# One decoder step (SSD, HGRN2 and two MLPs): the order of the engines' instructions comes from the scheduler's other machine model

## The chip, the cores and the metric

The kernel runs on one NeuronCore of one Trainium2 chip. Five engines work on it, each through its own list of instructions, in the order of that list: TensorE (PE, matrix products into PSUM), VectorE (DVE), ScalarE (ACT), GpSimdE (POOL) and SyncE (SP, which here only issues DMA transfers). They wait for one another through semaphores. The metric is the device time of one launch in microseconds (us), lower is better.

## The reference, cut to what matters

The step takes 512 prompt tokens of one new sequence and 32 sample tokens (8 sequences of 4 tokens), each a row of 1024 numbers, through two layers in float32:

```
h = x
h += ssd_mixer(rmsnorm(h))        # 32 heads of 64, 4 groups, state 64x128 per head
h += squared_relu_mlp(rmsnorm(h)) # 1024 -> 4096 -> 1024
h += hgrn_mixer(rmsnorm(h))       # 8 heads of 128
h += squared_relu_mlp(rmsnorm(h))
y = rmsnorm(h)
```

`ssd_mixer` multiplies by a 1024 x 5152 matrix, runs a causal convolution of width 4 and a SiLU over 3072 of the columns, scans the result along time in chunks (decays as differences of a cumulative sum, products inside a chunk, a state carried from chunk to chunk), multiplies by SiLU of a gate z, normalises each of 4 groups and multiplies by a 2048 x 1024 matrix. `hgrn_mixer` multiplies by 1024 x 4096, scans per head with a forget gate for each key dimension, normalises each head, gates and multiplies by 1024 x 1024. The new states are outputs too.

## The kernel before, in words

All 544 tokens (512 + 32) stay on chip; activations lie with features on the 128 partitions and tokens along the row, in 8 tiles `x[k]` of 128 x 544. The weights stream through in **units** of 128 x 1024: `raw<u>` is loaded by SP (L171) into one of three buffers, then split into a rounded part `whi` (ACT, L188 or L209) and a remainder `wlo` (DVE, L189; every third unit of the first layer on ACT and POOL, L230 and L233). A product runs as three passes, high x high, high x low and low x high, so a unit is 48 matmuls (L316, tiles `ps`, `po`, `pm`, `pd`, `pho`). Each product of a unit fills one of only **two** PSUM accumulators (`acc_tile`, pool `psb`, bufs=2): the product of unit n+2 cannot start until something has read the product of unit n. In the MLPs seven half-size products (L1020) stand for eight.

In the SSD layer the units come in the order of a list (ORDER, L35): gate units z (read by ACT `thz`, L511, and then by DVE `zs`, L512), input units i (read by three ACT copies into `pre`, L472 to L474, under high priority) and output units o (added to `x`, L405). After `pre` come `cacc` (ACT L480, three DVE steps L482), `th` (ACT L485) and the result (`xs`, `BC`, L486 and L489). `cacc` has one buffer, `pre` and `th` two.

Between the matmuls of the units runs **background** work, written as generators that give way after so many matmuls (PACE, L38): `scan` for each of 4 groups g, `gated_norm` behind it, and in the HGRN layer `levels` (tiles `pa`, at spans 1, 2, 4 ... 64 of a head) and `states` (`pk`, `pS`, `pz`, `po`, `pn`, `pt`). In `scan`, `rows(c)` has SP load a broadcast of the cumulative sums into `w<g>_<c>` (512 KB in 4 KB rows), and `weights(c)` turns it into decays on ACT: two L574 (`E`, only for c > 0), eight L576, one L577. `w`, the sample states `st`, and `bm` share six buffers of the tag "st", so a load of a `w` can have to wait until a state has been written out (L753) or until a matmul has read an older tile.

```
rows:     w = pool.tile([P, 8, P], F32, tag="st", bufs=6, ...)          # L563
          nc.sync.dma_start(w, cum_d[hs, c * P : (c + 1) * P].partition_broadcast(P))   # L564
weights:  nc.scalar.activation(w[:, h], w[:, h], AF.Relu, ...)          # L576, 8 times
          nc.scalar.activation(w, w, AF.Exp, scale=-1.0)                # L577
silu2:    nc.scalar.activation(v3(th), z, AF.Tanh, scale=0.5)           # L511
          nc.vector.scalar_tensor_tensor(v3(zs), v3(th), 1.0, z, ADD, MUL)   # L512
```

At the end of the HGRN layer the chain of the last head (7) runs `pa7_8`, `pa7_16`, `pa7_32`, `pa7_64` (L1159, L1178), `pk7` (L1250), `pS7` (L1262), `pz7`, `po7` (L1285, L1287), the norm of the head (`o`, `oms`, `nwr`, L1293 to L1302), `pt7` (L1316), `g7`, `oh7` and `ol7`, and then the output products `pho1_*` that read `oh7` and `ol7`. The output products of heads 0 to 3 are `pho0_*`.

The program traces all of this in Python order. Then the tile framework's scheduler sorts the instructions of each engine: it walks through a model of the machine, picks the next instruction that the model says can start, with the traced order and the priorities (`tc.high_priority()`) behind it, and sets semaphore waits to fit. What each engine runs, and on which tiles, is fixed by the trace; where each instruction stands in its engine's list is the scheduler's. The context that does this is opened in `_build`, L1536.

Of the kernel before, what the change touches and what calls it, by code (L numbers as in the profile page):

```python
# [1528 lines left out]
def _build(arrays):  # L1529
    import concourse.bacc as bacc  # L1530

    nc = bacc.Bacc("TRN2", target_bir_lowering=False, num_devices=1)
    io = {n: nc.dram_tensor(f"in_{n}", v.shape, mybir.dt.from_np(v.dtype), kind="ExternalInput").ap() for n, v in arrays.items()}
    for n, s in _OUT.items():
        io[n] = nc.dram_tensor(f"out_{n}", s, F32, kind="ExternalOutput").ap()
    with tile.TileContext(nc) as tc:  # L1536
        trunk(tc, io)
    return nc

# [21 lines left out]
```

## Time and profile before

| what | value |
|---|---|
| median of 3 runs | 1568.02 us (1567.37 to 1571.41) |
| the profiled execution, its own time | 1573.07 us |
| its span, first to last instruction | 1571.3 us |
| mean granted TensorE clock | 0.991 |
| PE busy | 1541.0 us, 98% of the span |
| DVE busy | 1092.6 us, 70% |
| ACT busy | 769.5 us, 49% |
| POOL busy | 121.0 us, 8% |

In the profile "L316" is line 316 of the kernel; "out<-in" names the tiles that an instruction writes and reads, without their numbers. A wait is the idle time of an engine just before an instruction, with what released it. "PEclk" is the clock that the throttle granted TensorE, 1.00 being full speed. Times in a timeline count from the start of the span. Windows give the busy time of each engine in a stretch.

### The profile page before, as it was taken

The page shows a single profiled execution, that of the slowest core. Times are in us where ns is not written, and L with a number is a line of the kernel's source. Part 1 is how long each engine was busy: PE and PEld are TensorE (multiplying, and loading weights), DVE is VectorE, ACT ScalarE, POOL GpSimd, SP SyncE. Part 2 cuts the span into 40 slices and gives each one's busy share as a digit, 9 for nine tenths or more (in the row PEclk, how much of TensorE's full clock was granted, in tenths as well). Part 3 has the DMA queues.
Part 4 walks back from the last instruction along what each step waited for, and adds up shares of the span by engine and source line. Part 5 has one row for each costly group of instructions (what it writes and reads, how often), then busy time and mean ns, then how long its engine had stood idle before and what let it go on. Part 6 is the DMA issues. An engine that isn't in the chain of part 4 may idle for free.

```text
span 1571.3 us, 32703 instructions
## 1 busy us (share of the span) xinstructions
PE 1541.0 (98%) x13420; PEld 1478.6 (94%) x13420; DVE 1092.6 (70%) x2142; ACT 769.5 (49%) x1506; POOL 121.0 (8%) x195
## 2 busy tenths in 40 slices
PE   8998899999999999999999999999999999999997
PEld 7997889898999999999999999999999999999996
DVE  7888797969778656464555878888878656474544
ACT  5686666675345436273554333333345446273552
POOL 4211010100001001010000000000001001010001
PEclk9999899999999999999999999999999999999998
DMA  6465456474446245453323232233226245363311
GB/s 195 123 172 161 131 140 180 121 215 123 139 100 174 90 118 148 111 161 92 110 63 108 69 99 83 89 105 110 70 91 180 81 128 141 108 167 94 103 55 58
DMA packets 86342, 188.94 MB, mean 120 GB/s; under 512 B 12784, under 2 KB 33168, under 8 KB 86192
## 3 DMA queue, kind: packets, MB, share of 16 engines
q1 hardware_dynamic: 73120, 164.21, 33.2%
q0 software_dynamic: 11808, 21.50, 8.6%
q8 instruction: 105, 1.72, 0.5%
q10 hardware_dynamic: 1264, 1.14, 0.2%
q14 instruction: 45, 0.37, 0.1%
HBM read 169.64 MB, written 17.18 MB: 119 GB/s over the span
## 4 chain that ended last, share of the span: by engine, by line
PE 87%; DMA 2%; DVE 2%; ACT 1%; issue 1%; POOL 0%; POOLq 0%; SPq 0%; ACTq 0%
PE pd L316 24%; PE ps L316 23%; PE pp L1020 11%; PE pm L316 6%; PE po L316 5%; PE pc L1020 5%; PE pho L316 3%; DMA w<-cum_d 1%; PE pa L1159 1%; PE py L608 1%; DMA raw<-in_W 1%; PE pu L599 1%; PE pi L620 1%; DVE wlo L189 1%; PE pS L1262 1%
## 5 line engine op out<-in xcount | busy, mean ns | idle before, releaser
L188 ACT CAST whi<-raw 128x512 fp32r<-128x512 f32 x318 | 195.1, 618 | 396.3 <-PE pd L316 155.2
L189 DVE TENSOR_TENSOR wlo<-raw,whi 128x512 fp32r<-128x512 f32 x318 | 218.4, 689 | 101.3 <-ACT whi L188 99.0
L316 PE MATMUL pd<-gh,whi 128*128 128x272 f32 x992 | 205.8, 288 | 0.0
L316 PE MATMUL pd<-gl,whi 128*128 128x272 f32 x992 | 205.3, 288 | 0.0
L316 PE MATMUL pd<-gh,wlo 128*128 128x272 f32 x992 | 205.1, 288 | 0.0
L316 PEld LDWEIGHTS pd<-gh,whi 128*128 128x128 f32 x992 | 156.0, 188 | 0.0
L316 PEld LDWEIGHTS pd<-gh,wlo 128*128 128x128 f32 x992 | 155.7, 188 | 0.0
L316 PEld LDWEIGHTS pd<-gl,whi 128*128 128x128 f32 x992 | 155.5, 188 | 0.0
L316 PE MATMUL ps<-uh_s,whi 128*128 128x272 f32 x576 | 127.0, 302 | 8.8 <-DVE zs L512 8.7
L316 PE MATMUL ps<-ul_s,whi 128*128 128x272 f32 x576 | 122.4, 294 | 0.0
L316 PE MATMUL ps<-uh,whi 128*128 128x272 f32 x512 | 112.6, 300 | 0.0
L316 PEld LDWEIGHTS ps<-uh_s,whi 128*128 128x128 f32 x576 | 92.9, 194 | 14.9 <-issue 13.2
L316 PE MATMUL ps<-ul,whi 128*128 128x272 f32 x512 | 106.5, 289 | 0.0
L316 PE MATMUL ps<-uh,wlo 128*128 128x272 f32 x512 | 106.2, 289 | 0.0
L405 DVE TENSOR_TENSOR x<-pd,x 128x544 f32<-128x544 f32 x62 | 44.8, 723 | 87.8 <-PE pd L316 87.8
L316 PEld LDWEIGHTS ps<-ul_s,whi 128*128 128x128 f32 x576 | 93.2, 194 | 0.3
L181 POOL DMA_DIRECT2D v<-in_W x48 | 42.1, 1068 | 599.7 <-DMA v<-in_W 373.4
L316 PE MATMUL ps<-uh_s,wlo 128*128 128x272 f32 x576 | 86.1, 290 | 0.0
L316 PEld LDWEIGHTS ps<-uh,whi 128*128 128x128 f32 x512 | 80.8, 189 | 3.7 <-issue 1.4
L316 PEld LDWEIGHTS ps<-ul,whi 128*128 128x128 f32 x512 | 80.4, 189 | 0.0
L316 PEld LDWEIGHTS ps<-uh,wlo 128*128 128x128 f32 x512 | 80.1, 188 | 0.0
L316 PEld LDWEIGHTS ps<-uh_s,wlo 128*128 128x128 f32 x576 | 78.3, 190 | 0.2
(428 smaller groups left out, 3810.4 us busy)
## 6 DMA issues: line engine op xcount, KB each, us to landing
raw<-in_W SPq DMA_DIRECT2D x198, 512.0 KB, 3.6
v<-in_W SPq DMA_DIRECT2D x48, 256.0 KB, 4.4
v<-in_W POOLq DMA_DIRECT2D x48, 256.0 KB, 5.6
wlo<-in_W POOLq DMA_DIRECT2D x34, 256.0 KB, 5.9
w<-cum_d SPq DMA_DIRECT2D x16, 512.0 KB, 7.3
st<-in_ssm_in SPq DMA_DIRECT2D x16, 512.0 KB, 5.5
out_ssm_s<-st SPq DMA_DIRECT2D x16, 512.0 KB, 4.9
a<-in_W SPq DMA_DIRECT2D x24, 256.0 KB, 4.0
```

The lines of the kernel that those rows point to most:

```text
L181: nc.gpsimd.dma_start(raw[:, c : c + 512], io["W"][u + 1][:, :512], accum_op=ADD)
L188: nc.scalar.copy(hi, raw)
L189: (eng or nc.vector).tensor_tensor(lo, raw, hi.bitcast(F32), SUB)
L316: nc.tensor.matmul(ps[:, h, :HF], block(a, c0 + k * step), o[:, h * HF : (h + 1) * HF], start=(first and i == 0), stop=(last and i == len( ...
L405: nc.vector.tensor_tensor(v3(x[m]), ps[:, :, :HF], v3(x[m]), ADD)
L599: nc.tensor.matmul(pu, bt[:, c], xts[c].rearrange("p h q -> p (h q)"), start=True, stop=True)
L608: nc.tensor.matmul(py[64 * (h % 2) : 64 * (h % 2) + 64, (h // 2) * P : (h // 2 + 1) * P], xds[c][:, h], ws_[c][:, h], start=True, stop=True,)
L620: nc.tensor.matmul(pi[:, j * P : (j + 1) * P], hT[:, j * P : (j + 1) * P], CT[:, cs], start=True, stop=True)
L1020: nc.tensor.matmul(ps, block(w, k * P), o, start=(name_ in ("p1", "p2", "q7") and k == 0 and j == 0), stop=(k == 3 and j == 2), skip_group ...
L1159: nc.tensor.matmul(pv4[b * NS : (b + 1) * NS, c], K[:, bs], QQ[:, 2 - n :, bs], start=True, stop=True, tile_position=(0, b * NS),)
L1262: nc.tensor.matmul(pS[:, c * P : (c + 1) * P], kt[:, c], vt[:, c], start=True, stop=True)
```

## The change

One argument is added where the tile context is opened:

```diff
-    with tile.TileContext(nc) as tc:
+    with tile.TileContext(nc, schedule_with_timeline_sim=True) as tc:
```

With it the scheduler uses its second machine model, which follows the engines' queues in time, to decide which instruction of an engine comes next. The instructions and their tiles are the same; each engine runs the same set, in another order, and the semaphore waits follow that order. Rows of PE change in 4858 lines of difference on some 6600 rows, of ACT in 1581 on some 1370. Three places follow; in the rows the number behind a unit's name (ps14) is the unit, or the group and chunk (w1_0), and the last number only tells buffers apart.

**ACT, in the SSD layer, around the copies of unit 14's product (pre17)**, which free the accumulator that unit 16's product (ps16) takes. Before:

```order
L188 CAST whi16_1_1707<-raw16_1434 128x512
L726 ACTIVATE bm0_1627<-bq0_1597,seqrow_123 128x128
L472 COPY pre17_1686<-ps14_1566 128x272
L473 COPY pre17_1686<-ps14_1566 128x240
L474 COPY pre17_1686<-ps14_1566 128x8x4
L726 ACTIVATE bm0_1627<-bq0_1597,seqrow_123 128x128
L480 ACTIVATE cacc7_1549<-pre7_1542,vh_129 128x568
L726 ACTIVATE bm0_1627<-bq0_1597,seqrow_123 128x128 x3
L576 ACTIVATE w1_0_2131<-w1_0_2131,tok_754 128x128 x5
```

Now:

```order
L726 ACTIVATE bm0_1627<-bq0_1597,seqrow_123 128x128 x8
L188 CAST whi17_1_1807<-raw17_1560 128x512
L230 ACTIVATE wlo18_1814<-raw18_1704 128x1024
L720 ACTIVATE ws0_1602<-ws0_1602 32x256
L576 ACTIVATE w1_0_2131<-w1_0_2131,tok_754 128x128 x8
L577 ACTIVATE w1_0_2131<-w1_0_2131 128x1024
L472 COPY pre17_1686<-ps14_1566 128x272
L473 COPY pre17_1686<-ps14_1566 128x240
L474 COPY pre17_1686<-ps14_1566 128x8x4
```

The copies stood ahead of all work on w1_0 and now stand behind all nine instructions of it. On PE the matmuls py0_3, whose end lets the load of w1_0 be issued, stood ahead of the end of unit 14's product; now they stand behind the end of unit 15's, with only psi0 and two of pn0 between them and ps16.

**ACT, a little later, around thz16**, the first reader of unit 16's product; ps18 takes its accumulator. Before:

```order
L574 ACTIVATE E1_1_2255<-w1_1_2142 64x512 x2
L576 ACTIVATE w1_1_2142<-w1_1_2142,tok_754 128x128 x7
L188 CAST whi19_1_1992<-raw19_1804 128x512
L576 ACTIVATE w1_1_2142<-w1_1_2142,tok_754 128x128
L485 ACTIVATE th21_1799<-cacc21_1794 128x568
L511 ACTIVATE thz16_1893<-ps16_1818 128x544
L577 ACTIVATE w1_1_2142<-w1_1_2142 128x1024
L574 ACTIVATE E1_2_2382<-w1_2_2174 64x512 x2
```

Now:

```order
L574 ACTIVATE E1_2_2382<-w1_2_2174 64x512
L373 ACTIVATE ssq_94<-y0_1158 128x544
L574 ACTIVATE E1_2_2382<-w1_2_2174 64x512
L577 ACTIVATE w1_1_2142<-w1_1_2142 128x1024
L188 CAST whi19_1_1992<-raw19_1804 128x512
L576 ACTIVATE w1_2_2174<-w1_2_2174,tok_754 128x128 x8
L485 ACTIVATE th17_1698<-cacc17_1693 128x568
L577 ACTIVATE w1_2_2174<-w1_2_2174 128x1024
L480 ACTIVATE cacc21_1794<-pre21_1787,vh_129 128x568
L485 ACTIVATE th21_1799<-cacc21_1794 128x568
L511 ACTIVATE thz16_1893<-ps16_1818 128x544
```

thz16 stood behind the work on w1_1 and ahead of that on w1_2; now it stands behind both, and th17 and cacc21, which stood ahead of w1_1, have moved behind w1_2 as well.

**PE, at the end of the HGRN layer, in head 7's chain from pS7 on.** Before:

```order
L316 MATMUL pho0_2_0_14432<-oh3_10176,wlo154_1_14342 128x272 x2
L1262 MATMUL pS7_14457<-vt7_14166,kt7_14415 128x128 x4
L316 MATMUL pho0_2_1_14469<-oh0_10170,whi154_0_14339 128x272 x2
L316 MATMUL pho0_2_1_14469<-ol0_10171,whi154_0_14339 128x272 x2
L316 MATMUL pho0_2_1_14469<-oh0_10170,wlo154_0_14341 128x272 x2
L316 MATMUL pho0_2_1_14469<-oh1_10172,whi154_0_14339 128x272 x2
L316 MATMUL pho0_2_1_14469<-ol1_10173,whi154_0_14339 128x272 x2
L316 MATMUL pho0_2_1_14469<-oh1_10172,wlo154_0_14341 128x272 x2
L1272 MATMUL pz7_14482<-hst7_14408,qm7_14417 32x128 x8
```

Now:

```order
L316 MATMUL pho1_0_1_14671<-oh6_10182,wlo156_1_14549 128x272 x2
L1250 MATMUL pk7_14410<-ident_77,K7_13890 128x128 x4
L1262 MATMUL pS7_14457<-vt7_14166,kt7_14415 128x128 x4
L1272 MATMUL pz7_14482<-hst7_14408,qm7_14417 32x128 x8
L1275 MATMUL pz7_14482<-ident_77,K7_13890 128x128
L1285 MATMUL po7_14509<-vt7_14166,att7_13921 128x128 x2
L1287 MATMUL po7_14509<-S7_14462,q7_13800 128x128
L1285 MATMUL po7_14509<-vt7_14166,att7_13921 128x128
L1287 MATMUL po7_14509<-S7_14462,q7_13800 128x128
L1285 MATMUL po7_14509<-vt7_14166,att7_13921 128x128
L1289 MATMUL pzs7_14517<-zi7_14492,h_sel_10154 32x128
```

Where the matmuls of pho0 stood between the steps of head 7's chain, all of pho0 and the parts of pho1 that do not read head 7 now stand ahead, and the steps from pk7 to pts7 follow one another directly.

## The prediction

> **What bounds the kernel now.** I read the page first: busy times, the chain that ended last, the transfers.
>
> ```profile
> PE 1541.0 (98%) x13420; PEld 1478.6 (94%) x13420; DVE 1092.6 (70%) x2142; ACT 769.5 (49%) x1506; POOL 121.0 (8%) x195
> ...
> PE 87%; DMA 2%; DVE 2%; ACT 1%; issue 1%; POOL 0%; POOLq 0%; SPq 0%; ACTq 0%
> ...
> w<-cum_d SPq DMA_DIRECT2D x16, 512.0 KB, 7.3
> ```
>
> PE is busy for 1541.0 of 1571.3 us. The matmuls stay the same ones, so an order of instructions can give back at most the 30 us in which PE is idle, and can cost any amount: every place counts at which PE would wait. Next, PE's waits.
>
> ```profile
> PE ps L316 <- DVE zs L512: 8.7, 1, 8.7
> PE gn_pc L351 <- DVE ssq L377: 2.4, 2, 1.7
> PE ps L316 <- DVE xl L369: 2.2, 3, 1.5
> ...
> PE po L316 <- ACT pre L474: 0.8, 1, 0.8
> ```
>
> One wait stands out: 8.7 us before a unit's product, for `zs`, the reader that frees one of the two accumulators. What it costs beside itself shows in the windows around it and around the 1.7 us wait of `gn_pc`.
>
> ```profile
> 150.00:155.00 5.00, 1.80 (x15) 1.58 (x13) 0.00 (x0) 3.77 (x10) 0.00 (x0) 1.00 0.82 294
> 155.00:160.00 5.00, 0.00 (x0) 0.00 (x0) 4.79 (x11) 4.50 (x10) 0.00 (x0) 0.69 0.73 217
> 160.00:165.00 5.00, 3.78 (x17) 3.54 (x17) 3.68 (x6) 5.00 (x12) 0.00 (x0) 0.63 0.82 295
> 165.00:170.00 5.00, 5.00 (x32) 5.00 (x32) 3.01 (x14) 0.94 (x2) 0.00 (x0) 0.71 0.08 33
> 170.00:175.00 5.00, 5.00 (x41) 5.00 (x40) 1.44 (x3) 2.87 (x6) 1.25 (x2) 0.95 0.32 92
> ...
> 255.00:260.00 5.00, 5.00 (x26) 5.00 (x26) 2.24 (x12) 3.43 (x7) 0.52 (x3) 0.57 0.83 194
> 260.00:265.00 5.00, 5.00 (x44) 5.00 (x43) 2.29 (x4) 2.90 (x7) 0.00 (x0) 1.00 0.32 113
> ```
>
> The second last column but two is the granted clock. In 155 to 160 PE does nothing, and afterwards does 32 matmuls in 5 us where it does 44 at a clock of 1.00: over 160 to 175 the low clock costs some 3.3 us. The clock also falls around 255 (26 matmuls instead of 44, 2 us), after no more than the 1.7 us wait.
>
> Last, ACT and SP around that stall.
>
> ```profile
> 127.40 0.39 ACT L472 COPY pre<-ps 128x272 f32<-128x272 f32 x1
> 127.68 0.37 ACT L473 COPY pre<-ps 128x240 f32<-128x240 f32 x1
> 127.93 0.21 ACT L474 COPY pre<-ps 128x32 f32<-128x32 f32 x1
> ...
> 130.00 1.58 ACT L576 ACTIVATE w<-w,tok 128x128 f32<-128x128 f32 x5
> ...
> 133.01 1.06 ACT L577 ACTIVATE w<-w 128x1024 f32<-128x1024 f32 x1
> ...
> 151.18 1.28 ACT L574 ACTIVATE E<-w 64x512 f32<-64x512 f32 x2 [5.04 <-DMA w<-cum_d]
> ...
> 155.36 0.66 ACT L485 ACTIVATE th<-cacc 128x568 f32<-128x568 f32 x1
> 155.93 0.60 ACT L511 ACTIVATE thz<-ps 128x544 f32<-128x544 f32 x1
> ...
> 157.93 1.28 ACT L574 ACTIVATE E<-w 64x512 f32<-64x512 f32 x2 [0.45 <-DMA w<-cum_d]
> ```
>
> ```profile
> 125.69 0.38 SPq L564 DMA_DIRECT2D w<-cum_d  x1
> ...
> 138.03 0.34 SPq L753 DMA_DIRECT2D out_ssm_s<-st  x1
> ...
> 143.18 0.38 SPq L564 DMA_DIRECT2D w<-cum_d  x1
> ...
> 145.99 9.46 SPq L564 DMA_DIRECT2D w<-cum_d  x2
> ```
>
> ACT sat 5.04 us on the transfer of w1_1 (issued 143.18, in use at 151.18: 8.0 us) with thz16 behind it; ps18 started at 160.47, once thz16 and zs16 were through. So the stall of before is itself one of order: an engine's list is served in order, and an instruction that waits for a slow transfer holds up the one that frees an accumulator. The change is judged by that rule, place by place, with the durations above.
>
> **The change, place by place.** I walked the new lists by hand. Times below are the clock of the trace of before.
>
> *Start.* DVE now runs six `xn` and four `ul` steps before the zs3 that frees the accumulator of ps4:
>
> ```profile
> 33.28 2.17 DVE L546 SCALAR_TENSOR_TENSOR xn<-x,vec,sn_rb 128x544 f32<-128x544 f32 x3
> ...
> 39.17 0.72 DVE L532 TENSOR_TENSOR zs<-ps,sn_rb 128x544 f32<-128x544 f32 x1
> ```
>
> Between 32.64 and 39.17 stood 6.5 us of DVE work, now 9.8: two more `xn` (0.7 each), both zs of L538 (0.7 each) and one more `ul` (0.65), without a gap. ps4 started at 40.03, right behind zs3: **+3.3**.
>
> *Unit 13.* From the groups of instructions, the number behind the busy time being the mean in ns:
>
> ```profile
> L744 DVE TENSOR_TENSOR st<-st,dec 128x1024 f32<-128x1024 f32 x16 | 19.3, 1216 | 0.0
> L230 ACT ACTIVATE wlo<-raw 128x1024 fp32r<-128x1024 f32 x17 | 18.1, 1068 | 0.3 <-PE po L316 0.3
> ```
>
> The copies pre5, 9.8 us early before, now follow wlo15 (L230, 1.1 us), which waits for the end of unit 12. With the 0.7 us of the copies, **+1.8**.
>
> *Units 16 and 18.* py0_3 now ends at 133.4. w1_0 is issued then, takes its 4.3 us (125.69 to 130.00) and is there at 137.8. ACT's nine instructions on it take 3.5 (130.00 to 134.07 less a 0.6 cast), the pre17 copies 0.7: 142.0. PE has 2.3 us of work behind py0_3 (psi0, two pn0) and wants ps16 at 135.6: a stall of 6.4. DVE now runs all four L744 (1.2 each) ahead of the additions into st0_0, so its write-out goes at 144.0 instead of 138.03; at the same 5.1 us (138.03 to the issue of w1_1 behind it) it lands at 149.2, w1_1 is issued and lands at 157.1. w1_2 goes at 149.7, held by pn0_7, and at the 11.9 us that the chain of waits gives it
>
> ```profile
> 145.99 11.91 DMA w<-cum_d
> ```
>
> it lands at 161.6. ACT then has, in its new order, E1_1, eight L576, cacc17, a cast (to 162.4), E1_2, ssq, L577, a cast, eight L576, th17, L577, cacc21 (to 170.8), waits for three DVE steps of 0.8, th21, thz16; DVE does BC1_5 and zs16. ps18 starts at 175.7 instead of 160.47: **+15.2** for both stalls together. gn0_pc no longer waits 0.7: **-0.7**. The clock falls after 8.7 us of idleness, so I let it fall after the 6.4 of ps16 too; of its 3.3 us some 0.8 lies beside the transfers: **+2.5**. The fall behind ps18 is in the time of before.
>
> Bounds: with w1_1 and w1_2 at 4.3 us, the shortest seen of this transfer here, ps18 starts at 172.0, +11.5 in place of +15.2; at 11.9 for both, 179.7, +19.2. A cost below nothing would need the same ACT work in front of thz16 to be shorter, and it is 18.5 us from E1_1 to zs16 where it was 9.2. I take the durations of the same transfers, since they stand among the same neighbours on SP.
>
> *Later in the SSD layer.* po0_2_1 waited 0.8 for pre18; the copies now follow E2_2 (1.3) and the square behind L776: a stall of 3.8, while the 1.7 of gn1_pc goes: **+1.3**, its clock fall replaced. In group 2, E3_2 and seven L576 (3.4) come ahead of pre19, which was 1.5 early: **+1.9**. The end of the layer, with gn3_pr 3.7 later on PE and two casts ahead of rb: **+1.6**; the three norms behind it (m0, hn, m1), each 2.7 to 3.1 later: **+3.4**. These are estimates from shifts of 2 to 4 us against the slack in the trace; each could be nothing.
>
> *The end of the HGRN layer.* In the trace nothing waits here; PE fills head 7's chain with pho0:
>
> ```profile
> 1124.00:1144.00 20.00, 20.00 (x229) 19.00 (x228) 15.68 (x34) 5.52 (x11) 0.00 (x0) 1.00 0.33 107
> 1144.00:1162.00 18.00, 18.00 (x152) 16.84 (x151) 13.32 (x37) 5.07 (x11) 0.00 (x0) 1.00 0.31 92
> ```
> ```profile
> 1128.16 0.42 DVE L1189 TENSOR_TENSOR q<-q,T 128x256 f32<-128x256 f32 x1
> 1128.49 0.42 DVE L1190 TENSOR_TENSOR K<-K,T 128x256 f32<-128x256 f32 x1
> ...
> 1149.26 0.82 DVE L1296 TENSOR_REDUCE oms<-o 128x5 f32<-128x640 f32 x1 [1.26 <-ACT o L1294]
> ...
> 1150.32 0.17 DVE L339 TENSOR_SCALAR nwr<-oms 128x5 int32<-128x5 int32 x1
> ...
> 1153.58 0.69 DVE L1299 TENSOR_TENSOR o<-po,nwr 128x512 f32<-128x512 f32 x1
> ...
> 1158.98 0.73 DVE L189 TENSOR_TENSOR ol<-g,oh 128x544 fp32r<-128x544 f32 x1 [0.71 <-ACT oh L188]
> ```
>
> From pa7_16 to the last product with head 7 PE now has only some 10 us of work, most of it the chain itself. Its waits: 1.5, 0.5 and 1.9 before pa7_16, pa7_32 and pa7_64 (q and K of the level, behind x, wlo, vm, g6 on DVE), 0.9 for the copy of pk7, 0.1 for S. Behind po7: square 0.7, seven hst steps now ahead of the reduction (2.0), reduction 0.8, eleven dependent small steps of 0.2 (2.2), two products 1.0, less 0.5 of pn7 on PE: 6.2. Then g7 and oh7 1.8, ol7 0.2. Sum **+13**. Below: if the levels' DVE steps run ahead (they need no PE result but the level before), only the norm and g7 remain, 8. Above: the clock falls here too, 16.
>
> *MLPs and the tail.* Each hop between PE and the readers keeps the slack that it had, so 0; without it each of 8 groups would pay tenths.
>
> **Sum**, against the profiled execution's own 1573.07: 3.3 + 1.8 + 15.2 - 0.7 + 2.5 + 1.3 + 1.9 + 1.6 + 3.4 + 13 = 43.3, so 1616.4. That execution lies 5.05 above the median of the runs shown, 1568.02; against the median the forecast is **1611 us**.
>
> **A rule beside it.** The clock fell both after 8.7 us and after 1.7 us of waiting. The Trainium skill ("TensorE: Matmul & The Clock Gate", section "The HAM clock gate") says that TensorE's clock goes to half after an idle window of about 3.4 us and comes back after as long a busy one. The trace agrees at 155 and does not at 255, where 1.7 us (0.8 before it) was enough. By that rule the falls here are those I count; by the row of 255 every wait of mine above 1.5 us brings one, a rival below.
>
> **Rivals.**
>
> *The clock falls at every wait and transfers queue longer.* For it: 0.57 at 255; 11.9 us for one w. Falls of 2 to 3.3 at the start, unit 13, group 2 and HGRN, some 9, and 4.0 from the transfers: 1624. Against it: the waits in HGRN are broken up by matmuls.
>
> *Only the SSD layer pays.* HGRN's chain hides behind slack that I don't see, DVE being busy 13.32 of 18 us there, and the small norm terms are nothing: 1611 - 13 - 5.0 = 1593.
>
> *Nothing to be seen.* The lists differ, but engines that run ahead make up for it, as 51% of ACT is idle: 1568. Against it: an accumulator has one reader, with its place in one list.
>
> *Faster.* The other model knows queues, so it spreads what waits: the 8.7 wait and its 3.3 of clock, gn_pc's 2.4 with its 2.0, go without a new one: 1568 - 16.4 = 1552. It decides if w1_2 has landed before ACT's list reaches E1_2, that is, within some 4 us of its issue, and py0_3 early enough. Against it: thz16 stands behind two transfers now, where it stood behind one.
>
> **How the numbers follow.** Forecast (1611) 0.57; clock and transfers (1624) 0.13; SSD only (1593) 0.14; nothing 0.06; faster 0.10. A measurement of this kernel can tell 0.3%, 4.7 us, from no change. Slower is 0.57 + 0.13 + 0.14 = 0.84, same 0.06, faster 0.10. The forecast's own bounds: below, 11.5 for the stall, 8 for HGRN and nothing for the five small later terms, 43.3 - 3.7 - 5 - 8.2 = 26, so 1594; above, +4.0 and +3, 1618. With the first two rivals the range is 1588 to 1630; outside it lie faster, nothing and a little of either end, 0.2.
>
> **What would show it.** Right: PE idle in front of ps16 (released by `pre`, ACT waiting for w before it) and ps18 (by `zs`), 6 and 17 us; idle of 6 us in front of pt7 and 2 in front of the last pho1; 3 before ps4; a clock below 0.8 twice between 135 and 200. PE's busy time up only by the clock. Wrong: the longest wait for `zs` below 9 us, or no PE wait near pt7; then the lists were read right and the lateness of transfers or of DVE was not.

## The result, and the profile after

| | before | after |
|---|---|---|
| median | 1568.38 us (1567.37 to 1571.41) | 1609.47 us (1606.69 to 1610.15) |
| the profiled execution, its own time | 1573.07 us | 1610.15 us |
| its span | 1571.3 us | 1608.4 us |
| mean granted TensorE clock | 0.991 | 0.979 |

The changed kernel is slower by 41 us: ratio 1.0253, 95% interval 1.0237 to 1.027. The forecast was 1611 us, with 1588 to 1630 as its range.

The page of after, its busy times and the granted clock in 40 slices:

```profile
PE 1541.4 (96%) x13420; PEld 1487.0 (92%) x13420; DVE 1091.5 (68%) x2142; ACT 769.9 (48%) x1506; POOL 121.4 (8%) x195
...
PEclk9998899999999999999999999999979999999998
```

PE is busy for as long as before (1541.0 us), in a span that is 37 us longer. The clock is lower in slices 4 and 5 (120 to 201 us) and in slice 30 (1166 to 1206 us). PE's waits in after, the costliest first (total, times, longest):

```profile
PE ps L316 <- DVE cm L688: 11.5, 1, 11.5
PE ps L316 <- ACT pre L474: 9.0, 2, 7.2
PE pt L1316 <- DVE o L1299: 5.6, 1, 5.6
PE fn_pr L1406 <- DVE nwr L344: 4.3, 2, 3.7
PE po L316 <- DVE x L405: 4.2, 2, 3.2
PE pc L1020 <- ACT fh_q L188: 4.0, 6, 1.0
PE ps L316 <- DVE zs L532: 3.2, 1, 3.2
PE pm L316 <- DVE a L1002: 2.5, 2, 1.5
...
PE pa L1178 <- DVE K L1190: 1.9, 2, 1.4
...
PE pa L1159 <- DVE K L1190: 1.7, 1, 1.7
PE pho L316 <- ACT oh L188: 1.4, 1, 1.4
```

The first line is the wait before ps18 (its releaser, `cm`, is the small DVE step right behind zs16). The second holds ps16 for 7.2. The `pt`, `pa` and `pho` lines are head 7's chain. The `pc` line (six short waits) lies in the MLPs, where the prediction expected nothing. The others are the places that it names at the start, at po0_2_1 and at the norms.

To see where the 37 us lie I laid PE's matmuls of both traces in order of time, and compared the times at which the same amount of work had been issued (a matmul's work is its spacing in the trace of before). The difference is called the **lag** below; where it grows, that stretch lost time.

| stretch | predicted | change of the lag, after |
|---|---|---|
| start and unit 13 | 3.3 + 1.8 | +6.5 |
| ps16 to ps19 (stalls, clock, gn0_pc) | 15.2 + 2.5 - 0.7 | +11.5 |
| po0_2_1, gn1 | 1.3 | -0.4 |
| group 2 | 1.9 | -1.1 |
| end of the SSD layer | 1.6 | +3.1 |
| norms m0, hn, m1 | 3.4 | +4.1 |
| bodies of the two MLPs | 0 | -3.0 |
| body of the HGRN layer | 0 | -3.6 |
| end of the HGRN layer | 13 | +18.8 |
| tail | 0 | +1.3 |
| sum | 43.3 | 37.2 |

### The profile page after: what moved, and what is told of

It reads as the page before. It is cut to its first block, busy times and chain, and to the rows that moved or that the text cites. A ratio compares the mean times of both kernels' runs of the same rounds, so it can differ in the third digit from the quotient of the medians.

```text
span 1608.4 us, 32657 instructions
## 1 busy us (share of the span) xinstructions
PE 1541.4 (96%) x13420; PEld 1487.0 (92%) x13420; DVE 1091.5 (68%) x2142; ACT 769.9 (48%) x1506; POOL 121.4 (8%) x195
## 4 chain that ended last, share of the span: by engine, by line
PE 86%; DVE 4%; DMA 4%; ACT 3%; issue 2%; POOL 0%; SPq 0%; POOLq 0%; ACTq 0%; DVEq 0%
PE ps L316 26%; PE pd L316 23%; PE pp L1020 8%; PE pm L316 6%; PE po L316 5%; PE pc L1020 3%; PE pho L316 3%; DMA raw<-in_W 3%; PE pa L1159 1%; PE py L608 1%; DVE wlo L189 1%; PE pu L599 1%; PE pd L1385 1%; DMA w<-cum_d 1%; PE pi L620 1%
## 5 line engine op out<-in xcount | busy, mean ns | idle before, releaser
L316 PE MATMUL ps<-uh_s,whi 128*128 128x272 f32 x576 | 127.9, 303 | 23.7 <-DVE cm L688 11.5
L316 PE MATMUL ps<-uh,wlo 128*128 128x272 f32 x512 | 109.8, 292 | 0.0
```

Of the source, the lines that this page charges most:

```text
L316: nc.tensor.matmul(ps[:, h, :HF], block(a, c0 + k * step), o[:, h * HF : (h + 1) * HF], start=(first and i == 0), stop=(last and i == len( ...
```

## Experiments

Every kernel below computes the whole reference. Each opens the context as the change does, but holds some or all engines to a given list, by a dependency between neighbours in that list that only sets the order:

```diff
         trunk(tc, io)
+        for names in lists:                    # one list for each engine
+            for prev, i in zip(names, names[1:]):
+                tc.add_manual_dep(i, prev, DependencyInfo(NoSync, DATA))
```

So a list, or one place of it, can be exchanged while the rest stays. In the short diffs the lists are told, not printed.

### One layer at a time

ssd_new, hgrn_new and mlp_new hold the engines to the lists of before, with the instructions of one part of the program put in the changed order:

```diff
-all engines: SSD layer, MLPs and norms, HGRN layer as before
+ssd_new:  SSD layer in the changed order
+hgrn_new: HGRN layer in the changed order
+mlp_new:  MLPs, norms m0 and m1, tail in the changed order
```

> The SSD layer's instructions stand in the changed order on every engine, all others in the order of before. Theory (each stage of the program pays for its own order, and the profiles of before and after are right stage by stage): +18 to +20 us on before, the loss that the profile of after shows up to the end of that layer (ps16 9.9, the start 6, the layer's end 3.3, ps18 and the rest near nothing). Rival 1 (the prediction's own terms for this layer, 15.2 for the two stalls with long transfers): +27. Rival 2 (the stages are coupled, the loss of one hides in the other): under +14.

> Only the HGRN layer's instructions stand in the changed order. Theory: a gain of about 3 us in the body of the layer (fewer switches between unit products and small matmuls) and a loss of 18.8 at its end, +14 to +16.5 in all. Rival 1 (the prediction's term for the end alone, body nothing): +13. Rival 2 (the loss at the end comes from the lateness that the SSD layer hands on): under +8.

> Only the two MLPs and the norms ahead of them (m0, m1) and behind (final) stand in the changed order. Theory: +2 to +5 us, from the waits of about 1.0 to 1.5 us at the norms and 1.2 at the tail that the profile of after shows. Rival (the waits of after in the MLPs, six at fh_q of up to 1.0 us, add to it): +7 to +9.

| | median | before beside it | ratio, 95% interval |
|---|---|---|---|
| ssd_new | 1591.30 us | 1571.34 us | 1.0125 (1.0105 to 1.0145) |
| hgrn_new | 1585.71 us | 1571.34 us | 1.0089 (1.0062 to 1.0115) |
| mlp_new | 1570.62 us | 1571.34 us | 1.0001 (0.9985 to 1.0018) |

PE's waits of ssd_new, and then those of hgrn_new:

```profile
PE ps L316 <- DVE cm L688: 11.5, 1, 11.5
PE ps L316 <- ACT pre L474: 8.9, 2, 7.1
```
```profile
PE ps L316 <- DVE zs L512: 6.5, 1, 6.5
PE pt L1316 <- DVE o L1299: 5.6, 1, 5.6
```

The same waits as in after appear, each with its own layer and nowhere else. The SSD layer costs 20.0 us (the theory's 18 to 20, not the prediction's 27). The HGRN layer costs 14.4 (its interval, some 10 to 18, holds the rival's 13 too), and its lag has the two parts foretold, which tell it from that rival: -2.6 in the body, +18.2 at the end. (Its trace shows a wait for ps18 of 6.5 where before had 8.7, in an order that is the same there: that stall varies by some 2 us with the transfers; the load of w1_1 took 5.7 us there and 7.9 in before.) mlp_new missed its +2 to +5: the medians differ by nothing. Its lag shows why: +1.6 and +1.3 at the two norms, and -0.8 and -1.3 in the two MLP bodies. What the bodies gain from was not settled. The three differences of medians add up to 33.6 us where after lost 41; by the traces the sum is nearer, 18.3 + 15.6 + 0.9 = 34.8 of 37.1. Within that, the layers are independent. And mlp_new, which opens the context, holds every engine to a list and keeps both mixer layers in the order of before, takes the time of before: what costs is the order alone.

### The two stalls of the SSD layer

The changed kernel, with one place put back, then both:

```diff
 ACT (pre17b)
+L472 L473 L474 pre17<-ps14
 L576 w1_0 x8, L577 w1_0
-L472 L473 L474 pre17<-ps14
 DVE (pre17b)
 L482 cacc6, second step
+L482 cacc6, third step
 L622, L605, L189, L744 st0_0, L721, L744 st0_1
-L482 cacc6, third step
```
```diff
 ACT, and their steps on DVE (thzup)
+L480 cacc7, L472-L474 pre21, L485 th7, L480 cacc17, L485 th17, L480 cacc21
 L574 E1_1 x2, L576 w1_1 x2
+L485 th21
 L576 w1_1 x2
+L511 thz16
 L576 w1_1 x4, L574 E1_2 x2, L577 w1_1, L576 w1_2 x8, L577 w1_2
-(those, where they stood between and behind)
 DVE (thzup), among others
-L752 st0_0, second
 L486 L489 xs1_2, L482 cacc7, first step
+L482 cacc7, second and third step, L486 L489 xs1_3, L752 st0_0, second
```

So in thzup thz16 stands ahead of all work on w1_2, but still behind E1_1, which reads w1_1, and behind four of the eight L576 on w1_1.

> The changed order, with the copies of unit 14's product (pre17) put back ahead of ACT's work on w1_0, and on DVE the third step on cacc6, which frees the buffer that pre17 is written to, ahead of the L744 behind which it stood. Theory: the 7.2 us wait in front of ps16 and the 2.7 of low clock behind it go, but the load of w1_1 still goes out behind the write-out of st0_0 at 153.4, so E1_1 and with it thz16 come only some 3 us earlier and the wait in front of ps18 grows by some 7: -2 to -5 us on the changed kernel, 1604.5 to 1607.5. Rival (the two stalls are independent): -9 to -11, 1598.5 to 1600.5.

> The changed order, with the chain that leads to the reader of unit 16's product (cacc7, pre21, th7, cacc17, th17, cacc21, th21, thz16 on ACT and their steps and zs16 on DVE) moved up as far as the data allow, so that thz16 no longer stands behind the work on w1_1 and w1_2. Theory (what holds ps18 is the place of thz16 in ACT's list, not the transfers): the 11.5 us wait in front of ps18 and some 2 to 3.3 of low clock go, -11 to -15 us on the changed kernel, 1594.5 to 1598.5. Rival (the transfers of w1_1 and w1_2 hold PE in any order): -4 to +1.

> The changed order with both repairs of the SSD layer together: pre17's copies ahead of the work on w1_0, and the chain to thz16 and zs16 moved up. Alone they gave about -4 and -5 us on the changed kernel, since each let PE run into the next wait (the wait for ps18, 3.2 us for gn0_pc's ssq). Theory (the two stalls are coupled: one's removal only moves PE to the other): together more than the sum, -14 to -19 us, 1590.5 to 1595.5. Rival (a third limit stands behind both, the arrival of w1_1 and the steps of group 0 that wait for PE): no more than the sum, -6 to -10, 1599.5 to 1603.5.

| | median | against after's 1609.47 us | ratio to before, 95% interval |
|---|---|---|---|
| pre17b | 1605.46 us (before beside it 1568.72) | -4.0 | 1.022 (1.0193 to 1.0247) |
| thzup | 1603.82 us (1568.72) | -5.7 | 1.0216 (1.0192 to 1.0241) |
| fix2, both | 1604.00 us (1568.21) | -5.5 | 1.0239 (1.0223 to 1.0255) |

The intervals of all three overlap with that of after (1.0237 to 1.027), so the times alone hardly tell a repair from after; what each did is read from the traces.

Each repair did at its place what it was to do. In pre17b ps16 starts at 143.35 us instead of 149.98, in thzup ps18 starts at 173.25 instead of 179.78. But PE's waits show what came next; pre17b, thzup and fix2 in this order:

```profile
PE ps L316 <- DVE cm L688: 11.5, 1, 11.5
...
PE pn L751 <- DVE y L612: 2.2, 1, 2.2
```
```profile
PE gn_pc L351 <- DVE ssq L377: 3.2, 1, 3.2
```
```profile
PE pn L751 <- DVE st L752: 5.9, 1, 5.9
PE gn_pc L351 <- DVE ssq L377: 5.8, 1, 5.8
```

In pre17b PE waits for DVE's `y` and then as long as ever before ps18, which starts only 2.3 us earlier (177.47). In thzup the wait goes to gn0_pc, whose squares on ACT still stand behind the work on w1_2. With both, PE waits 5.9 us for the states and 5.8 us for the squares. The first of these is the repair's own doing: the second L752 on st0_0 now stands on DVE behind the steps of cacc7 and xs1_3. It also sends out st0_0, and behind it the load of w1_1, 6 us later than in after (159.43 us in fix2, 159.89 in thzup, 153.39 in after). So the expectation of pre17b held (-2 to -5), thzup's fell between its two, and fix2 is its rival's case, half a us outside its range: not more than the sum of the two, but a third limit behind both. As one part of that limit was put there by the repair, what the two stalls alone are worth stays open. ps19 starts at 186.72, 186.81 and 186.25 us in the three, and at 189.76 in after: whichever wait is removed, these orders let group 0 through at about the same time.

### The end of the HGRN layer

hspread takes the changed order and moves the scans of the heads up against the products of the units:

```diff
 PE, DVE, ACT, POOL, HGRN layer
-scan steps of head h (pa, pk, pS, pz, po, pn, pt, norm) as in the changed order
+the same steps up to 17 us earlier against the products, growing along the layer
```

> The changed order, but in the HGRN layer the work of the heads' scans on PE, DVE, ACT and POOL is moved up against the products of the units, by nothing at 880 us and linearly up to 17 us at 1167 us, as far as the data allow; products, casts of weights and additions to x keep their order. Theory (the changed order lets the scans fall almost a head behind the products, so that the products that could fill the waits of head 7 are used up before it): head 7's waits of 11.3 us and the low clock behind them shrink to a few us, -10 to -17 us on the changed kernel, 1592.5 to 1599.5. Rival (DVE, busy 80 to 93% in the layer, or the chain itself sets the end, whatever PE has to fill it): -4 to +4.

It took 1620.36 us (before beside it 1568.72), 11 us more than after: neither the theory's -10 to -17 nor the rival's -4 to +4. The lag tells the two halves apart. At the end of the layer it grows by 8.4 us, where after's grows by 18.8: with the scans further on, head 7's chain does cost less there. But in the body of the layer the lag grew by 16.8 us, where after's fell by 3.6. (Another 3 us went in the MLP ahead, where a wait for `fh_q` rose to 2.1; that was not followed up.) PE's waits in hspread, and its clock at one of them (the columns are those of the prediction's windows; the third from the end is the granted clock):

```profile
PE pt L1316 <- DVE o L1299: 8.1, 2, 4.4
...
PE pa L1159 <- DVE K L1190: 2.7, 1, 2.7
```
```profile
1100.00:1110.00 10.00, 9.02 (x60) 8.18 (x61) 7.50 (x14) 1.78 (x4) 0.89 (x2) 0.66 0.01 3
```

One of the two `pt` waits (3.7 us) is now another head's, at 1101, with the clock at 0.66 behind it: a norm that is moved nearer to its transposes makes PE wait there. So the theory's first half fits (the end costs what it does because the scans lag and the filling products are used up), and its second half, that moving them up is free, is refuted. Which spacing of the lists has neither loss, as before's has, was not found. PE's list of this layer alone, or the others' alone, was not tried in the new order: the lists of the engines wait for one another and fit only together.

### The clock, and the cost of changing between kinds of matmuls

gn1late holds everything to the order of before and moves one pair of norm products on PE:

```diff
 PE
 L316 ps28 x5
-L351 gn1_pc x5
 L316 ps28 x19
+L351 gn1_pc x5
 L316 ps28 x20
-L360 gn1_pr x5
 L316 ps28 x4, po0_3_0 x12
+L360 gn1_pr x5
 L583 pxt2_0
```

> The order of before, with the first norm product of group 1 (gn1_pc) 19 product matmuls later on PE, so that it no longer waits, and the second (gn1_pr) 16 later. Theory (the clock fell around 255 because PE waited 0.8 and 1.7 us there): the wait of 1.7 us and the 2 us of low clock both go, -3 to -4 us, and the granted clock from 250 to 260 is above 0.95. Rival 1 (the clock falls there for another reason, so a wait under about 3.4 us costs its own length alone): -1.2 to -1.8, with the clock still below 0.7 somewhere from 250 to 260. Rival 2 (nwr comes no sooner, so gn1_pr waits instead): -1 to +1.

The window of before ahead of the one that the prediction shows, then those of gn1late over the same place and behind it, and the wait that gn1late meets there:

```profile
250.00:255.00 5.00, 3.30 (x19) 3.28 (x19) 4.50 (x10) 3.83 (x8) 1.76 (x2) 0.75 0.51 162
```
```profile
250.00:255.00 5.00, 5.00 (x44) 5.00 (x43) 4.29 (x14) 4.71 (x12) 2.00 (x4) 1.00 0.57 134
255.00:260.00 5.00, 5.00 (x45) 5.00 (x44) 2.66 (x9) 3.75 (x8) 0.27 (x1) 1.00 0.90 205
...
270.00:275.00 5.00, 4.95 (x28) 4.96 (x29) 4.44 (x8) 3.54 (x9) 0.00 (x0) 0.66 0.01 3
```
```profile
PE pcb L651 <- DVE BC L486: 1.9, 1, 1.9
```

The 1.7 us wait is gone, the clock stays at 1.00, and PE does 45 matmuls in 255 to 260 instead of 26. From the start of po0_2_1 (246.13 us in before, 244.59 here) to that of the second `pxt` of group 2 (267.48 and 260.85) the lag falls by 5.1 us: the wait, and 3.4 us of clock. The theory and the prediction had 2 us for the clock, from the window 255 to 260 alone, but the fall began in the window before it (0.75). Then PE, now earlier, waits 1.9 us for group 2's `BC`, with a clock of 0.66 behind it, and 3.6 of the 5.1 are gone. The time did not fall by the 3 to 4 us of the theory: the median is 1570.66 against 1568.21 (ratio 1.0018, 1.0002 to 1.0034), though its profiled execution is 3.1 us shorter than that of before. The gain is lost some 10 us later, and not to gn1_pr, as rival 2 had it. That the wait brings the fall is borne out here, but it does not bring it each time: hgrn_new has the order of before in this layer and the same wait of 1.7 us, and keeps its clock.

```profile
255.00:260.00 5.00, 5.00 (x42) 4.98 (x41) 2.29 (x9) 4.33 (x11) 0.27 (x1) 1.00 0.92 210
```

split cuts small groups of matmuls in two:

```diff
 PE, HGRN layer, at 39 places
-small group x16; L316 x2
+small group x8; L316 x2; small group x8
```

> The order of before, with 39 of the small groups of matmuls in the HGRN layer (levels, transposes, states) on PE each cut in two by the two product matmuls that followed it: 197 changes between products and small matmuls become 275. Nothing else moves, and PE waits nowhere there in the kernel before. Theory (each change between the two kinds costs about 0.1 us, which is where the 2.6 to 3.6 us that the changed order gained in the body of the layer come from): +5 to +9 us. Rival (a change of kind costs nothing, the gain has another cause): -1 to +1.5.

It took 1577.50 us, before beside it 1568.21 (ratio 1.0068, 1.0053 to 1.0084). In the traces, from the start of ps121 (the layer's second product) to that of pm161 (the first product of the second MLP), before takes 330.6 us and split 340.6: +10.0 us for 78 more changes, 0.13 us each. PE waits nowhere in the stretch, in either, and the clock is 1.00. The rival (nothing) is refuted; the cost is a little above the theory's +5 to +9. The changed order has 27 changes fewer in this layer (170 against 197); at 0.13 us that is 3.5 us, enough for the 2.6 to 3.6 that its body gained.

### Versions that are faster than both

The prediction's rule (an instruction that waits for a transfer holds up the one that frees an accumulator) says how the order of before could be better, too:

```diff
 ACT (early16)
 L188 whi19_0
+L485 th21, L511 thz16, L373 ssq, L188 whi19_1, L376 gsq
 L574 E1_1 x2
+L376 gsq x2, L511 thz17, L188 whi20_0
 L576 w1_1 x4
+L188 whi20_1, L511 thz18
 L576 w1_1 x4, L577 w1_1, L574 E1_2 x2, L576 w1_2 x8, L577 w1_2
 DVE (early16): zs16 behind the third step of cacc21, both L767 and the first L776; L744, L752 of st0_3 later
 PE (early16): L351 gn0_pc behind ps18, not within it
+early16b: DVE: gn0's small steps ahead of wlo20_1 and zs18; PE: L360 gn0_pr 24 products later
+best3: early16b, gn1late, and pu1_0, py1_0, pi1_1, pu1_1, py1_1, pi1_2 on PE 12 products later
```

> The order of before, with ACT's and DVE's work between unit 16's and unit 19's products re-sorted: th21, thz16 and zs16 stand ahead of E1_1 (which waits for the transfer of w1_1), and thz17, thz18 ahead of the rest of the work on w1_1 and w1_2; the first norm product gn0_pc stands behind ps18. Theory (an instruction that waits for a transfer holds up the one that frees the accumulator; nothing else holds ps18): the 8.67 us wait, the 0.75 of gn0_pc and the 3.3 of low clock behind them go: -10 to -13 us on before, 1556 to 1558. Rival (the transfers hold PE anyway: the stall moves to the next product that needs w1_1 or a state): -4 to +1.

> As early16 (the order of before with th21, thz16 and zs16 ahead of E1_1), with the small steps of group 0's norm ahead of zs18 on DVE and its second norm product gn0_pr 24 matmuls later on PE. Theory: the 2.74 us wait for nwr that early16 put in the place of the old one goes as well, with the low clock behind it, -10.5 to -13 us on the kernel before, 1557 to 1560 against a before of 1570. Rival (another reader is late next): no better than early16's -8.

> early16b (the order of before with thz16 and zs16 ahead of the work on w1_1, and the norm's steps earlier) with gn1late, and with the first steps of group 1's scan on PE (pu1_0, py1_0, pi1_1, pu1_1, py1_1, pi1_2) each 12 product matmuls later, so that they meet their inputs. Theory (the 3.4 us waits for w and their low clock in early16b go, and gn1_pc's too): -13 to -17 us on the kernel before, 1552 to 1556 against a before of 1569. Rival (the next reader is late again): -5 to -9, like early16.

| | median | before beside it | ratio, 95% interval |
|---|---|---|---|
| early16 | 1562.15 us | 1571.34 us | 0.9948 (0.9932 to 0.9965) |
| early16b | 1564.04 us | 1568.72 us | 0.9972 (0.9957 to 0.9987) |
| best3 | 1561.45 us | 1568.21 us | 0.9967 (0.9954 to 0.998) |

early16's waits:

```profile
PE gn_pr L360 <- DVE nwr L344: 2.7, 1, 2.7
```

and best3's:

```profile
PE py L608 <- DVE w L631: 3.6, 2, 1.8
...
PE pcb L651 <- DVE BC L486: 1.9, 1, 1.9
```

The wait for zs16 of 8.7 us is gone in all three: ps18 starts at 152.49 us in early16, 160.47 in before, and the lag is down to -12.0 us soon after. But 2.7 us for `nwr`, with the clock behind it, take 4.4 of that back. early16b removes that wait and meets two others, 1.1 us for `bt` at 179 us and 2.0 for `w` at 182; best3 moves the steps that wait and still meets 1.8 for `w` at 185. (The other wait in the `w` line above, 1.7 us at 102, lies ahead of every place that was changed; before has 0.7 there, and early16b 1.4.) All three end some 5 to 9 us ahead of before (the products of the first units, which no list here changes, began up to 3 us apart from one profiled execution to the next, so the three are not told apart). early16 missed its -10 to -13 by little, and the two that did more are their rivals' case: what is late next was each time a few us away. All three are faster than both kernels, by 0.3 to 0.5% of before; early16 has the lowest ratio.

## Why the prediction was right, and which steps were not

The verdict and the place of the losses came as forecast, and the time within 2 us, but the last is in part luck. By the traces the sum should have been 37 us and was 43.3. Against it stands the 5.05 us that were taken off because the profiled execution of before lay so far above its median: that of after lay 0.7 above its own. The 6 us too much and the 4.4 too much taken off nearly cancel; within the sum, the terms of the SSD layer were too large and those of the HGRN layer too small.

**Start and unit 13** (3.3 + 1.8): PE waited 3.2 us for zs3, as said, and the two places came to 6.5 together instead of 5.1. The window of after behind that wait has the rest, a clock of 0.66:

```profile
45.00:50.00 5.00, 5.00 (x29) 5.00 (x29) 5.00 (x9) 3.17 (x6) 0.75 (x1) 0.66 0.37 107
50.00:55.00 5.00, 5.00 (x43) 5.00 (x42) 1.75 (x3) 0.62 (x1) 0.00 (x0) 1.00 0.12 16
```

With 29 matmuls where 43 fit at 1.00, 0.116 us each, that is some 1.6 us, which the first rival had.

**ps16.** The wait was 7.2 us (said: 6.4), released by `pre`, with ACT waiting for w1_0. ACT in after:

```profile
145.77 2.44 ACT L576 ACTIVATE w<-w,tok 128x128 f32<-128x128 f32 x8 [5.31 <-DMA w<-cum_d]
...
161.88 1.29 ACT L574 ACTIVATE E<-w 64x512 f32<-64x512 f32 x2 [0.33 <-PE pys L757]
...
178.09 0.60 ACT L511 ACTIVATE thz<-ps 128x544 f32<-128x544 f32 x1
```

and SP, with the loads of w1_0 and w1_1 and the write-out of st0_0 between them:

```profile
140.15 0.38 SPq L564 DMA_DIRECT2D w<-cum_d  x1
...
150.76 0.34 SPq L753 DMA_DIRECT2D out_ssm_s<-st  x1
153.39 0.38 SPq L564 DMA_DIRECT2D w<-cum_d  x1
```

w1_0 took 5.6 us (140.15 to 145.77; the walk had 4.3), the nine instructions and the copies followed it as walked.

**ps18, the term that was too large.** ps18 started at 179.78. The walk had 175.7, and the losses ahead of it 5.1, so 180.8: right within some 1 us, but by luck. The walk lets E1_1 wait for w1_1, 8.0 us behind its issue. w1_1 went out 2.6 us behind st0_0's write-out (said: 5.1) and landed 4.0 us later, at 157.4. E1_1 started only at 161.88, and it waited at last for PE's `pys`. The chain that ended with ps18, in order of time, shows what PE had done until then:

```profile
149.98 5.99 PE ps L316 x27
...
161.50 0.35 PE pys L757 x2
...
162.53 0.64 ACT E L574
```

PE ran from ps16 on without a pause, at a clock of 0.50 in 150 to 155 us, and its matmuls there took 2.4 us more than at 1.00. So the low clock lies inside the start of ps18: it took the place of the transfer that was shorter than said. pre17b bears it out: there PE does not wait for ps16 and has its full clock behind it, and E1_1 starts at 158.84, released by w1_1. From E1_1 to the end of zs16 ACT and DVE took 17.8 us (said: 18.5), and ACT waited in it for no transfer.

What was wrong is the sum around it: the low clock behind ps16 (+2.5) was added to a start of ps18 (+15.2) that, as measured, already has it. PE waited 11.5 us before ps18, not the 17 that the prediction gave as a sign. Up to behind ps18 the terms came to 22.1 us (5.1 + 15.2 + 2.5 - 0.7), and the lag there was 18.0: of the 4.1 too much, 2.5 are this clock, 1.0 is ps18's start, and 0.6 came back behind it. thzup and fix2 add what the prediction did not see: with thz16 moved up, other readers in the same lists were late at nearly the same time, some of them by that move.

**The smaller terms of the SSD layer.** po0_2_1 waited 3.2 us (said: 3.8), with a fall of the clock that cost 1.6 behind it. The 1.7 of gn1_pc went, and the fall behind it, which the prediction took as replaced, had cost 3.4. Together that is less than the 0.8, 1.7 and 3.4 of before: -0.4 by the table, instead of +1.3. Group 2 lost nothing (said: 1.9). The end of the layer lost 3.1 (said: 1.6). The norms lost 4.1 (said: 3.4).

**The end of the HGRN layer, the term that was too small.** The windows of after, and PE's timeline there:

```profile
1170.00:1175.00 5.00, 1.93 (x54) 1.54 (x55) 4.96 (x14) 1.16 (x3) 0.00 (x0) 0.74 0.22 88
1175.00:1180.00 5.00, 4.63 (x24) 4.27 (x24) 1.31 (x3) 0.70 (x2) 0.00 (x0) 0.58 0.00 0
...
1190.00:1195.00 5.00, 2.73 (x11) 2.30 (x12) 2.57 (x5) 0.64 (x1) 0.00 (x0) 0.50 0.00 1
1195.00:1200.00 5.00, 5.00 (x24) 4.77 (x24) 3.99 (x6) 3.00 (x5) 0.00 (x0) 0.53 0.16 25
```
```profile
1171.20 0.46 PE L1159 MATMUL pa<-q,K 128*32 128x32 f32 x32 [1.67 <-DVE K L1190]
...
1174.93 1.09 PE L1178 MATMUL pa<-q,K 128*64 128x64 f32 x8 [1.44 <-DVE K L1190]
...
1190.83 1.08 PE L1316 MATMUL pt<-ident,o 128*128 128x128 f32 x4 [5.64 <-DVE o L1299]
...
1193.60 1.27 PE L316 MATMUL pho<-oh,whi 128*128 128x272 f32 x4 [1.44 <-ACT oh L188]
```

The waits were much as walked: 1.7 and 1.4 at the levels (said: 1.5 and 1.9), 5.6 at pt7 (said: 6.2) and 1.4 at the last output products (said: 2.0). What the prediction left out of its likeliest case is the clock: it is 0.50 to 0.58 in three of the windows, and PE does 24 matmuls in 1195 to 1200 where it does 43 at 1.00. Over the matmuls of 1172 to 1200 us, the low clock comes to 6.2 us (their spacing less that of the same kinds in before) and the waits, with two short ones not shown, to 11.3: together 17.5 of the 18.8. The prediction's 13 was waits alone; the clock was left to its upper bound (16) and its first rival. The reason given against that rival, that the waits are broken up by matmuls, was wrong.

**The bodies of the layers** were taken at nothing and gained 6.6 us in all: 3.6 in HGRN, for which the fewer changes of kind are enough (27 at 0.13 us, by split), 3.0 in the MLPs, cause open. **The tail** lost 1.3 (said: nothing): `fn_pr` waits twice now, 3.7 us the longer.

**The rule beside it.** The Trainium skill ("TensorE: Matmul & The Clock Gate", section "The HAM clock gate") puts the fall of the clock behind an idle window of about 3.4 us. Here shorter waits brought it too, though not each time. gn1_pc's wait of 1.7 us stands in six traces: in before, early16, early16b, mlp_new and split the clock fell within 3 us behind it, in hgrn_new it did not. In gn1late and best3, which take the wait away, it did not fall there either. The wait of 1.8 us at unit 13 stands in six traces with the changed order and brought a fall in three (hspread, ssd_new, thzup), but not in after; that of 1.5 us at the norm m0 brought none in six. In all these traces the clock is either 1.00 or 0.50, and inside the span it stays low for 3.4 us or a multiple of it. The measurement decides: in this kernel a wait of 1.5 to 2 us is to be priced as a risk of a fall, and a fall with 1.7 us, or 3.4 where it lasts twice as long.

Of the rivals, faster did not come: thz16 stood behind ACT's work on w1_1 and w1_2, though ACT waited for neither transfer; "nothing to be seen" did not, because an accumulator's reader has its place in one list; "SSD only" fell by hgrn_new. The clock at every wait came true at the start and in the HGRN layer, but not at unit 13 (a wait of 1.8 us without a fall) nor at the norms, and the longer transfers not at all.

## What to carry to other kernels

Two stalls behind one another, and the low clock between them, are not simply added: work out from all engines, PE and its clock among them, the time at which each product can start, and take the loss once, at the last. Where the order of the lists is what costs, removing one wait moves PE to the next reader in the same lists, often within 10 us (fix2, gn1late, best3), so price a repair by what is late next and not by the wait that it removes, and look at what the repair itself puts later (fix2). And a scheduler's other order is judged at the places where the program has least to fill a chain with, here the end of a layer.

## What the hardware showed that was not expected

Each change between products of the units and small matmuls cost PE 0.13 us (split: 10.0 us for 78), with no wait in the profile. It can be seen in one place of after's PE timeline:

```profile
1166.71 0.42 PE L316 MATMUL pho<-ol,whi 128*128 128x272 f32 x2
1167.06 0.46 PE L1159 MATMUL pa<-q,K 128*32 128x32 f32 x32
1167.45 0.52 PE L316 MATMUL pho<-oh,wlo 128*128 128x272 f32 x2
1167.80 0.48 PE L316 MATMUL pho<-oh,whi 128*128 128x272 f32 x2
1168.11 0.41 PE L316 MATMUL pho<-ol,whi 128*128 128x272 f32 x2
1168.36 0.41 PE L316 MATMUL pho<-oh,wlo 128*128 128x272 f32 x2
```

The pairs of products start 0.25 us apart (1168.11 to 1168.36). The small group starts 0.35 behind the pair ahead of it, and behind it the first two pairs are 0.35 and 0.31 apart: 0.10, 0.10 and 0.06 too much, 0.26 for the two changes. The products take operands of type float32r and these small matmuls float32, and they differ in shape as well; which of these costs the time was not told apart.

The other thing is how short a wait can be and still be followed by a fall of the clock: behind 1.7 us, and small norm products, it was 0.75 and 0.57 over the two windows of 5 us in before, some 6.8 us at half. The same wait in hgrn_new had none.
